# Where the recurrence's outputs are transposed, and which engine scales P: a two-layer decoder kernel

## The chip, the cores and the metric

The kernel runs on one core of one Trainium2 chip. The metric is the device time of one execution in microseconds (us), lower is better. The core has TensorE (PE, matmuls; PEld is its weight loading), VectorE (DVE), ScalarE (ACT), GpSimd (POOL) and a queue for DMA issues on SyncE (SP). Each engine works through its own instructions in a fixed order and waits on semaphores for the others.

## What is computed

Two layers of a decoder trunk on one sequence of 512 tokens, 1024 wide, in float32. In each layer an RWKV-7 recurrence (8 heads of 64) and a latent attention (MLA, 8 heads) run on the same normalised input; their outputs are gated, added and projected, and a gated MLP with a short convolution follows. Cut to what the change touches:

```python
y = _wkv7_scan(r, decay, k, v, -kk, kk * iclr)            # recurrence, (tokens, 8 heads, 64)
mu = jnp.mean(y, axis=-1, keepdims=True)                  # group norm over the 64 of a head
var = jnp.mean(jnp.square(y - mu), axis=-1, keepdims=True)
y = (y - mu) * lax.rsqrt(var + LNX_EPS) * lnx_w + lnx_b
y_a = ((y + bonus) * gate) @ w_out_rwkv

s = (q_nope @ k_nope.T + q_pe @ k_pe.T) * scale           # attention, causal mask
p = jax.nn.softmax(s, axis=-1)
y_b = (p @ v) @ w_out_mla

merged = sigmoid(gate_a) * y_a + sigmoid(gate_b) * y_b
h = h + merged @ w_out
```

## The kernel before

**Layout and products.** Activations lie transposed, features on the 128 partitions and the 512 tokens along the free axis. A large product is made of three matmuls (`mm3`, L253 to L255): both operands are split into a high and a low part in the fp32r format, and high x high, low x high and high x low are summed in PSUM. Weights come as units of 128 x 1024 from HBM over SP's queue (`produce`, L211), into two buffers each for the raw, high and low parts; ScalarE makes the high part (L203) and VectorE the low one (L204). `unit` keeps two units ready ahead of use. Activations are split in the same way by `split` (L286 on ScalarE, L287 on VectorE).

**Stages of a layer** (`mixer`). First the input projections, with the preparation of the recurrence for four pairs of heads. Then the recurrence over eight half-chunks of 64 tokens. Then the part in which the change lies, and last the output projections and the MLP.

**The part around the change** runs these functions in this order, once a layer:

- `outputs`: for four chunks of 128 tokens, `chunk_out(i)` sums the outputs of all heads in the two-bank PSUM tile xy, of which there is a single buffer (matmuls L874 and L884), and ScalarE copies them to Z (L888).
- `norms`: for each chunk, `group_norm(i)` has VectorE sum each head's 64 values (L896), multiply the sums by 1/64 (L897) and subtract them (L898); ScalarE squares (L899), VectorE sums the squares (L900) and scales (L901), and GpSimd raises to the power -0.5 (L902). `group_scale` then multiplies Z on GpSimd (L907).
- `heads(p)`, four times, each for a pair of heads: the key projection (3 matmuls) is copied by ScalarE (L957) and completed by GpSimd (L958), the two query projections (12 matmuls) are scaled by VectorE (L965). For four blocks of 128 queries and two heads: scores on TensorE (L973), masking and row minimum of the negated scores on VectorE (L976), exp with row sums on ScalarE (L979), reciprocal on VectorE (L980), scaling of P by it on ScalarE (L981), up to four 128 x 128 transposes on TensorE (L984), and a copy of the turned P out of PSUM (L985), on ScalarE for blocks 1 and 3 and on VectorE for blocks 0 and 2. At the end 16 matmuls give P x V (L992), and the result is split.
- `transposed`, between the second and the third pair: four calls of `yop`, two to an xy tile. Each transposes 128 features of all four chunks (four L913), loads the bonus and the gate (L915, L917) into two rotating buffers that all four calls share, adds the transposed values times lnx_w to the bonus (L923, or two halves at L921 for the last two calls), multiplies by the gate (L924) and splits the result.

After the four pairs come eight products of all four split outputs with w_out_rwkv, each followed by a multiplication with the gate (L1005).

**What sets the order.** The order on each engine is fixed when the kernel is built. A scheduler goes by priority, which is the order in the program, and puts later work ahead of earlier work where the earlier isn't ready by its own reckoning. Only the stretches inside `manual_schedule` keep TensorE's order as written. So the place of `transposed` in the list of functions sets a rank, not a fixed place. The accumulators of the projections have two PSUM buffers, keys and queries five buffers in SBUF, P three.

Of the kernel before, what the change touches and what calls it, by code (L numbers as in the profile page):

```python
# [9 lines left out]
F32 = mybir.dt.float32  # L10
F32R = mybir.dt.float32r
I32 = mybir.dt.int32
AF = mybir.ActivationFunctionType
ALU = mybir.AluOpType
# [145 lines left out]
def build(ctx, tc, x, pos, wst, vecd, constd, out):  # L160
    nc = tc.nc
    V, A, G, PE = nc.vector, nc.scalar, nc.gpsimd, nc.tensor
# [270 lines left out]
    def mixer(l, ops, nrm, wks):  # L433
        with ExitStack() as mx:
# [245 lines left out]
            with pool(name=f"ti{l}", bufs=2) as ti, tc.manual_schedule(engines={PE.engine}):  # L680
# [130 lines left out]
                for c in range(8):  # L811
                    i, e = divmod(c, 2)
                    xy = xyt()
# [16 lines left out]
                    for hd in (0, 4, 1, 5, 2, 6, 3, 7):  # L830
                        s, ur, vr = slot(c, hd // 2)
                        g, n = divmod(hd, 4)
# [24 lines left out]
            with pool(name=f"tb{l}", bufs=2) as tb:  # L857
# [7 lines left out]
                def chunk_out(i):  # L865
                    xy = xyt()
                    begun, left = set(), {(r, hh): 4 for r in (0, 64) for hh in range(2)}
                    for p in range(4):
                        for e, hh in ((0, 0), (1, 1), (0, 1), (1, 0)):
                            c = 2 * i + e  # L870
                            s, ur, vr = slot(c, p)
                            k0 = 64 * hh
                            if c:
                                PE.matmul(xy[vr:vr + 64, hh, 64 * p:64 * p + 64], AR[p][k0:k0 + 64, s, vr:vr + 64],  # L874
                                          St[c][k0:k0 + 64, p, :], start=(vr, hh) not in begun, stop=False,
                                          tile_position=(k0, vr))
                                begun.add((vr, hh))
                    for hh in range(2):
                        for p in range(4):
                            for e in range(2):  # L880
                                s, ur, vr = slot(2 * i + e, p)
                                hd = 2 * p + hh
                                left[vr, hh] -= 1
                                PE.matmul(xy[vr:vr + 64, hh, 64 * p:64 * p + 64], AM[:, hd, s, vr:vr + 64],  # L884
                                          Z[:, i, e, 64 * hd:64 * hd + 64], start=(vr, hh) not in begun,
                                          stop=left[vr, hh] == 0, tile_position=(0, vr))
                                begun.add((vr, hh))
                    A.copy(Z[:, i, 0, :].rearrange("p (q h i) -> p q h i", h=2, i=64),  # L888
                           xy[:, :, 0:256].rearrange("p h (q i) -> p q h i", i=64))


                def group_norm(i):
                    Y = Z[:, i, 0, :].rearrange("p (h i) -> p h i", i=64)
                    s2 = Z[:, i, 1, :].rearrange("p (h i) -> p h i", i=64)
                    mu = tb.tile([128, 16], F32, name="mu", bufs=4)
                    V.tensor_reduce(mu[:, 0:8], Y, mybir.AxisListType.X, ALU.add)  # L896
                    V.tensor_scalar(mu[:, 0:8], mu[:, 0:8], 1.0 / 64, None, ALU.mult)  # L897
                    V.tensor_tensor(Y, Y, mu[:, 0:8, None].to_broadcast([128, 8, 64]), ALU.subtract)  # L898
                    A.activation(s2, Y, AF.Square)  # L899
                    V.tensor_reduce(mu[:, 8:16], s2, mybir.AxisListType.X, ALU.add)  # L900
                    V.tensor_scalar(mu[:, 8:16], mu[:, 8:16], 1.0 / 64, LNX_EPS, ALU.mult, ALU.add)  # L901
                    G.tensor_tensor(mu[:, 0:8], mu[:, 8:16], mhalf[:, 0:8], ALU.pow)  # L902
                    return mu[:, 0:8]
# [7 lines left out]
                def yop(ps, p):  # L911
# [12 lines left out]
                    V.tensor_tensor(bl, bl, gt, ALU.mult)  # L924
                    yops.append(split(xp, bl, None, "xa", 8))

                def outputs():
                    for i in range(4):
                        chunk_out(i)

                def norms():
                    for i, gr in enumerate([group_norm(i) for i in range(4)]):
                        group_scale(i, gr)

                def transposed():
# [15 lines left out]
                def heads(p):  # L951
# [8 lines left out]
                    for hh in range(2):  # L960
# [3 lines left out]
                        q = MT("q", "qk", 5)  # L964
# [3 lines left out]
                    PTs = [tb.tile([128, 13, 128], F32, name="PT", tag="PT", bufs=4) for _ in range(2)]  # L968
                    for b in range(4):
                        n = 128 * (b + 1)  # L970
                        for hh in range(2):
                            sp = sc()
                            PE.matmul(sp[:, 0:n], qs[hh][:, 128 * b:128 * b + 128], ks[hh][:, 0:n], start=True, stop=True)  # L973
                            P = MT("P", "P")
# [3 lines left out]
                                                   scalar=1e30, op0=ALU.add, op1=ALU.min, accum_out=mn[:, 0:1])  # L978
                            A.activation(P[:, 0:n], P[:, 0:n], AF.Exp, bias=mn[:, 0:1], scale=-1.0, accum_out=mn[:, 1:2])  # L979
                            V.reciprocal(mn[:, 2:3], mn[:, 1:2])  # L980
                            A.activation(P[:, 0:n], P[:, 0:n], AF.Copy, scale=mn[:, 2:3])  # L981
                            pt = pb.tile([128, 512], F32, name="pt", tag="pt")
                            for kb in range(b + 1):
                                PE.transpose(pt[:, 128 * kb:128 * kb + 128], P[:, 128 * kb:128 * kb + 128], ident)  # L984
                            (A.copy if b % 2 else V.tensor_copy)(PTs[hh][:, b:4 * b + 1:3, :],  # L985
                                                                 pt[:, 0:n].rearrange("p (k q) -> p k q", q=128))

                    with tc.manual_schedule(engines={PE.engine}):
# [5 lines left out]
                                          start=kb == 0, stop=kb == 3, tile_position=(0, 64 * hh))  # L994
                    oops.append(split(xp, po, None, "xb", 8))

                for f in (outputs, norms, lambda: heads(0), lambda: heads(1), transposed, lambda: heads(2), lambda: heads(3)):
                    f()

                gas = []  # L1000
# [151 lines left out]
```

## Time and profile before

| what | us |
|---|---|
| median of 3 runs | 1564.96 |
| lowest and highest | 1563.26, 1566.88 |
| the profiled execution: its time | 1565.82 |
| its span in the trace | 1564.0 |
| PE busy | 1532.7 (98%) |
| DVE busy | 913.5 (58%) |
| ACT busy | 669.2 (43%) |
| POOL busy | 184.4 (12%) |

The shares are means over the whole span, and most of it is large products that feed TensorE alone. The stage around the change takes from about 278 to 338 us in layer 0 and again from about 1050 to 1110 us in layer 1; only there do all engines work on one chain. A row of a wait names the engine, the tile and line that waited, the engine, tile and line that ended the wait, then the total, the number of times and the longest. A row of a time window gives its length and the busy time of PE, PEld, DVE, ACT and POOL with the numbers of their instructions, then the clock granted to TensorE as a share of full speed, the share of DMA time and the GB/s.

### The profile page before, as it was taken

What the parts mean: (1) busy time and instruction counts of PE and PEld (TensorE: products, weight loads), DVE (VectorE), ACT (ScalarE), POOL (GpSimd) and SP (SyncE); (2) the same over time, 40 slices, a digit from 0 to 9 for tenths busy, and PEclk for the clock granted to TensorE, in tenths of its full rate; (3) what the DMA queues carried; (4) which work ended last, traced back from release to release, by engine and by line L of the source; (5) the groups of instructions that cost most, each with busy time, mean ns of one, the idle gap of its engine ahead of it and who ended that gap; (6) DMA issues with size and microseconds to landing.
All of it is one profiled execution on the core that took longest, in us unless ns stands there. A gap on an engine that the chain in (4) does not pass through costs nothing.

```text
span 1564.0 us, 22128 instructions
## 1 busy us (share of the span) xinstructions
PE 1532.7 (98%) x8860; PEld 1233.0 (79%) x8860; DVE 913.5 (58%) x1510; ACT 669.2 (43%) x1020; POOL 184.4 (12%) x157
## 2 busy tenths in 40 slices
PE   8999999999999999999999999998999999999998
PEld 6888886668888888888878888765788888888887
DVE  6579795766555555533346768867564555554332
ACT  6445444663443333322244544457444333333222
POOL 1011101300311110100001121013012111100000
PEclk9999999999999999999999999999999999999999
DMA  6324322324323222333342333222352232222322
GB/s 208 115 95 139 124 83 69 96 86 155 122 89 101 95 95 94 100 116 115 108 149 94 109 108 117 81 65 92 101 171 92 96 106 95 94 95 96 103 98 81
DMA packets 57270, 166.05 MB, mean 106 GB/s; under 512 B 6352, under 2 KB 8528, under 8 KB 57168
## 3 DMA queue, kind: packets, MB, share of 16 engines
q1 hardware_dynamic: 57024, 164.48, 31.9%
q8 instruction: 69, 1.13, 0.3%
q14 instruction: 33, 0.27, 0.1%
q10 hardware_dynamic: 144, 0.16, 0.0%
HBM read 147.32 MB, written 17.30 MB: 105 GB/s over the span
## 4 chain that ended last, share of the span: by engine, by line
PE 92%; DVE 5%; ACT 1%; issue 1%; POOL 0%; DMA 0%; DVEq 0%; POOLq 0%; SPq 0%; ACTq 0%
PE acc L253 27%; PE acc L254 27%; PE acc L255 27%; PE sc L973 2%; PE pt L984 1%; PE po L992 1%; PE m L635 1%; DVE wlo L204 1%; PE xy L834 1%; PE m L643 1%; PE xy L844 1%; PE acc L947 1%; PE m L540 0%; DVE X L694 0%; DVE tm L692 0%
## 5 line engine op out<-in xcount | busy, mean ns | idle before, releaser
L253 PE MATMUL acc<-hi,whi 128*128 128x512 f32 (+1 forms) x1918 | 755.0, 394 | 6.1 <-ACT hi L289 5.2
L255 PE MATMUL acc<-hi,wlo 128*128 128x512 f32 (+1 forms) x1918 | 747.4, 390 | 0.8 <-DVE wlo L204 0.8
L254 PE MATMUL acc<-lo,whi 128*128 128x512 f32 (+1 forms) x1918 | 746.8, 389 | 0.0
L203 ACT CAST whi<-raw 128x1024 fp32r<-128x1024 f32 (+2 forms) x249 | 253.4, 1019 | 535.8 <-PE acc L254 463.3
L253 PEld LDWEIGHTS acc<-hi,whi 128*128 128x128 f32 x1918 | 361.2, 188 | 81.4 <-ACT hi L289 5.2
L255 PEld LDWEIGHTS acc<-hi,wlo 128*128 128x128 f32 x1918 | 361.2, 188 | 75.4 <-DVE wlo L204 1.3
L254 PEld LDWEIGHTS acc<-lo,whi 128*128 128x128 f32 x1918 | 361.5, 188 | 71.1 <-DVE lo L290 0.5
L204 DVE TENSOR_TENSOR wlo<-raw,whi 128x1024 fp32r<-128x1024 f32 (+2 forms) x249 | 303.3, 1220 | 178.2 <-ACT whi L203 177.8
L1072 POOL TENSOR_TENSOR c<-c,rstd 128x512 f32<-128x512 f32 x44 | 57.9, 1317 | 403.6 <-ACT c L1071 403.6
L1065 DVE TENSOR_TENSOR u<-acc,rstd 128x512 f32<-128x512 f32 x44 | 30.4, 692 | 104.4 <-PE acc L255 104.3
L1074 DVE TENSOR_TENSOR c<-c,acc 128x512 f32<-128x512 f32 x44 | 30.2, 687 | 86.4 <-POOL c L1072 86.4
L1071 ACT ACTIVATE c<-c 128x512 f32<-128x512 f32 x44 | 27.8, 632 | 81.7 <-DVE c L1070 81.7
L312 POOL TENSOR_TENSOR nv<-nv,cst 128x4 f32<-128x4 f32 (+1 forms) x10 | 10.0, 996 | 335.4 <-DVE nv L311 335.4
L348 POOL TENSOR_TENSOR nacc<-nacc,nsq 128x512 f32<-128x512 f32 x14 | 25.1, 1790 | 193.0 <-ACT nsq L347 193.0
L973 PE MATMUL sc<-K,q 128*128 128x128 f32 (+3 forms) x128 | 45.4, 451 | 1.3 <-DVE mn L976 1.0
L466 DVE TENSOR_TENSOR cur<-acc,rstd 128x512 f32<-128x512 f32 x28 | 19.1, 689 | 45.1 <-PE acc L255 37.6
L981 ACT ACTIVATE P<-P,mn 128x128 f32<-128x128 f32 (+3 forms) x64 | 35.1, 559 | 5.1 <-DVE mn L980 4.8
L979 ACT ACTIVATE P<-P,mn 128x128 f32<-128x128 f32 (+3 forms) x64 | 35.5, 556 | 3.7 <-DVE mn L976 3.5
L1068 ACT ACTIVATE c<-u,vec 128x512 f32<-128x512 f32 x44 | 35.7, 811 | 2.8 <-DVE u L1064 2.8
L976 DVE CUSTOM_DVE_ANT_0 P<-sc,cst 128x128 f32<-128x128 f32 (+3 forms) x64 | 30.4, 482 | 8.1 <-PE sc L973 5.5
L1070 DVE SCALAR_TENSOR_TENSOR c<-u,vec,c 128x512 f32<-128x512 f32 x44 | 33.1, 752 | 1.5
L1069 DVE SCALAR_TENSOR_TENSOR c<-u,vec,c 128x512 f32<-128x512 f32 x44 | 32.8, 746 | 1.8 <-ACT c L1068 1.8
(243 smaller groups left out, 1318.5 us busy)
## 6 DMA issues: line engine op xcount, KB each, us to landing
raw<-in_w SPq DMA_DIRECT2D x238, 512.0 KB, 3.3
gate_d<-gg SPq DMA_DIRECT2D x32, 256.0 KB, 2.0
AM<-gate_d SPq DMA_DIRECT2D x16, 256.0 KB, 4.2
gb<-gate_d SPq DMA_DIRECT2D x16, 256.0 KB, 3.2
h<-in_x SPq DMA_DIRECT2D x8, 256.0 KB, 4.3
rgate_d<-gt SPq DMA_DIRECT2D x8, 256.0 KB, 2.5
bl_d<-rk SPq DMA_DIRECT2D x8, 256.0 KB, 4.2
bl<-bl_d SPq DMA_DIRECT2D x8, 256.0 KB, 2.6
```

Of the source, the lines that this page charges most:

```text
L203: A.copy(hi, r)
L204: V.tensor_tensor(lo, r, hi.bitcast(F32), ALU.subtract)
L253: PE.matmul(ps, w[0], xx[0], start=first, stop=False)
L254: PE.matmul(ps, w[0], xx[1], start=False, stop=False)
L255: PE.matmul(ps, w[1], xx[0], start=False, stop=last)
L973: PE.matmul(sp[:, 0:n], qs[hh][:, 128 * b:128 * b + 128], ks[hh][:, 0:n], start=True, stop=True)
L979: A.activation(P[:, 0:n], P[:, 0:n], AF.Exp, bias=mn[:, 0:1], scale=-1.0, accum_out=mn[:, 1:2])
L981: A.activation(P[:, 0:n], P[:, 0:n], AF.Copy, scale=mn[:, 2:3])
L1068: A.activation(cc, u[:, 2:514], AF.Identity, bias=vc(l, "conv_b", i), scale=vc(l, "conv_w", 2 * FT + i))
L1069: V.scalar_tensor_tensor(cc, u[:, 1:513], vc(l, "conv_w", FT + i), cc, ALU.mult, ALU.add)
L1070: V.scalar_tensor_tensor(cc, u[:, 0:512], vc(l, "conv_w", i), cc, ALU.mult, ALU.add)
L1072: G.tensor_tensor(cc, cc, rstd, ALU.mult)
```

## The change

Three edits, all in the part described above.

1. `transposed` is called behind `heads(2)` and no longer behind `heads(1)`.
2. The sums for the group norm's means are taken by VectorE straight from the PSUM tile xy in `chunk_out`, beside ScalarE's copy, and no longer from Z. The multiplication of the sums by -1/64 and the subtraction become one operation.
3. The scaling of P by the reciprocal is a `tensor_scalar` on VectorE and no longer an activation on ScalarE, and all copies of the turned P are made by ScalarE.

```diff
@@ chunk_out
+                    mu = tb.tile([128, 16], F32, name="mu", bufs=4)
+                    V.tensor_reduce(mu[:, 0:8].rearrange("p (q h) -> p h q", h=2),
+                                    xy[:, :, 0:256].rearrange("p h (q i) -> p h q i", i=64), mybir.AxisListType.X, ALU.add)
                     A.copy(Z[:, i, 0, :].rearrange("p (q h i) -> p q h i", h=2, i=64),
                            xy[:, :, 0:256].rearrange("p h (q i) -> p q h i", i=64))
+                    return mu
@@ group_norm
-                def group_norm(i):
+                def group_norm(i, mu):
-                    mu = tb.tile([128, 16], F32, name="mu", bufs=4)
-                    V.tensor_reduce(mu[:, 0:8], Y, mybir.AxisListType.X, ALU.add)
-                    V.tensor_scalar(mu[:, 0:8], mu[:, 0:8], 1.0 / 64, None, ALU.mult)
-                    V.tensor_tensor(Y, Y, mu[:, 0:8, None].to_broadcast([128, 8, 64]), ALU.subtract)
+                    V.scalar_tensor_tensor(Y, mu[:, 0:8, None].to_broadcast([128, 8, 64]), -1.0 / 64, Y, ALU.mult, ALU.add)
@@ outputs, norms
+                sums = []
+
                 def outputs():
                     for i in range(4):
-                        chunk_out(i)
+                        sums.append(chunk_out(i))
 
                 def norms():
-                    for i, gr in enumerate([group_norm(i) for i in range(4)]):
+                    for i, gr in enumerate([group_norm(i, sums[i]) for i in range(4)]):
                         group_scale(i, gr)
@@ heads
                             V.reciprocal(mn[:, 2:3], mn[:, 1:2])
-                            A.activation(P[:, 0:n], P[:, 0:n], AF.Copy, scale=mn[:, 2:3])
+                            V.tensor_scalar(P[:, 0:n], P[:, 0:n], mn[:, 2:3], None, ALU.mult)
...
-                            (A.copy if b % 2 else V.tensor_copy)(PTs[hh][:, b:4 * b + 1:3, :],
+                            A.copy(PTs[hh][:, b:4 * b + 1:3, :],
@@ the order
-                for f in (outputs, norms, lambda: heads(0), lambda: heads(1), transposed, lambda: heads(2), lambda: heads(3)):
+                for f in (outputs, norms, lambda: heads(0), lambda: heads(1), lambda: heads(2), transposed, lambda: heads(3)):
```

## The prediction

> **What bounds the kernel now.** I read the page first (the chain that ended last, then the costliest groups), then who waited for whom on TensorE, then time windows over the stage in which the change lies, and last its timeline.
>
> ```profile
> PE 92%; DVE 5%; ACT 1%; issue 1%; POOL 0%; DMA 0%; DVEq 0%; POOLq 0%; SPq 0%; ACTq 0%
> PE xy L913 <- POOL Z L907: 4.0, 2, 2.0
> PE pt L984 <- DVE mn L980: 1.7, 2, 0.8
> PE xy L874 <- ACT Z L888: 1.6, 4, 0.6
> PE sc L973 <- DVE mn L976: 1.0, 2, 0.5
> PE xy L913 <- DVE bl L921: 0.9, 2, 0.5
> ```
>
> TensorE carries 92% of the chain, so an edit on another engine is worth only what it takes from TensorE's idle or slow time. The waits (total, times, longest) fall in equal halves on the two layers, all in the stage that the change touches. Layer 0's stage, from the end of the second pair's projections to the last pair, in thirds (length; busy PE, PEld, DVE, ACT, POOL; clock):
>
> ```profile
> 290.00:306.00 16.00, 13.93 (x67) 10.25 (x66) 12.80 (x38) 11.61 (x29) 6.12 (x6) 0.89 0.21 67
> 306.00:322.00 16.00, 14.07 (x72) 8.27 (x70) 12.42 (x39) 13.26 (x33) 0.61 (x1) 1.00 0.24 66
> 322.00:338.00 16.00, 16.00 (x86) 9.62 (x85) 10.23 (x31) 11.87 (x29) 0.00 (x0) 1.00 0.16 47
> ```
>
> TensorE is idle for 2.07 us in the first third and 1.93 us in the second, and runs at 0.89 clock in the first (0.11 x 16 = 1.8 us lost). The last third is full: there the products with the recurrence's output weights fill the holes of the last pair. ScalarE (13.26 of 16) is the busiest of the helpers in the second third, VectorE (12.80) in the first. One microsecond at a time, the first third shows:
>
> ```profile
> 290.00:291.00 1.00, 0.37 (x3) 0.13 (x1) 0.86 (x4) 0.00 (x0) 1.00 (x1) 1.00 0.00 0
> 291.00:292.00 1.00, 0.00 (x0) 0.00 (x0) 1.00 (x4) 0.63 (x1) 0.92 (x2) 1.00 0.00 0
> 293.00:294.00 1.00, 1.00 (x5) 0.76 (x4) 0.93 (x5) 0.30 (x1) 0.48 (x1) 0.62 0.00 0
> 294.00:295.00 1.00, 1.00 (x5) 0.80 (x4) 0.25 (x2) 0.78 (x2) 1.00 (x1) 0.50 0.00 0
> 295.00:296.00 1.00, 1.00 (x3) 0.60 (x3) 0.43 (x1) 1.00 (x3) 0.92 (x2) 0.50 0.00 0
> 296.00:297.00 1.00, 1.00 (x3) 0.46 (x3) 1.00 (x1) 0.91 (x4) 0.28 (x1) 0.67 0.00 0
> ```
>
> The transposes (L913) stand in TensorE's queue ahead of work that could run, wait 2.0 us for GpSimd's scaling of Z, and just behind that the clock is at half for some three microseconds. Both belong to one event.
>
> **Part 1: the transposes move behind pair 2.** The function issues 16 transposes, 8 loads on SP's queue, 6 VectorE steps on the transposed data (two of 0.73 us, four halves), four products with the gate, and four splits. None goes away; all now rank behind pair 2's work, which takes TensorE and VectorE first. Where the transposes stood, pair 2's 15 projection matmuls can run, which need nothing from the norms. So the wait of 2.0 us goes (a) and with it the slow clock, 1.8 us (b). What is late next is the end of the outputs' own chain, since the products at the end need all four:
>
> ```profile
> 297.89 0.73 DVE L923 SCALAR_TENSOR_TENSOR bl<-xy,vec,bl 128x512 f32<-128x512 f32 x1
> 302.00 0.69 DVE L965 TENSOR_TENSOR q<-acc,rq 128x512 f32<-128x512 f32 x1
> 306.87 2.37 PE L992 MATMUL po<-PT,Vt 128*64 128x512 f32 x16
> 322.12 2.37 PE L992 MATMUL po<-PT,Vt 128*64 128x512 f32 x16
> 323.20 0.62 ACT L286 CAST hi<-bl 128x512 fp32r<-128x512 f32 x1 [0.85 <-DVE bl L924]
> 323.85 0.69 DVE L287 TENSOR_TENSOR lo<-bl,hi 128x512 fp32r<-128x512 f32 x1 [0.22 <-ACT hi L286]
> 328.85 0.79 PE L253 MATMUL acc<-hi,whi 128*128 128x512 f32 x1
> 319.68 0.32 SPq L917 DMA_DIRECT2D rg<-rgate_d  x1
> 322.48 0.68 DVE L924 TENSOR_TENSOR bl<-bl,rg 128x512 f32<-128x512 f32 x1
> 322.59 13.98 SPq L211 DMA_DIRECT2D raw<-in_w  x2
> DMA to landing us min/median/max: 2.6/2.7/3.9
> ```
>
> The chain runs from 297.89 to 324.54, 26.65 us. The fourth output is first used by the matmul at 328.85: 4.3 us of slack. The two buffers of loads set its pace (the last gate's load is issued at 319.68, when a buffer comes free, and its product follows at 322.48, the 2.7 us of a landing later). The delay lies between nothing (the transposes find holes at once) and one pair, 322.12 - 306.87 = 15.25 us. I take 6, nearer the low end: in before pair 2's projections were done at 302.00, 4.1 us behind the chain's start, and its first scores come behind them. That costs 6 - 4.3 = 1.7 us (e), with ends 0 and 10.9. On SP's queue, which is worked in order, the next weights (322.59) come behind the last gate load; a load that waits longer for its buffer holds them back too. I put nothing on it: here the weights were issued 2.9 us behind that load, and the code keeps two units of weights ready ahead of use.
>
> **Part 2: the scaling of P to VectorE, the copies of turned P to ScalarE.** Eight scalings for a pair of heads, four copies of each of the two kinds.
>
> ```profile
> L981 ACT ACTIVATE P<-P,mn 128x128 f32<-128x128 f32 (+3 forms) x64 | 35.1, 559 | 5.1 <-DVE mn L980 4.8
> L985 DVE COPY PT<-pt 128x384 f32<-128x384 f32 x16 | 8.8, 552 | 1.6 <-PE pt L984 1.5
> L985 DVE COPY PT<-pt 128x128 f32<-128x128 f32 x16 | 4.6, 286 | 3.4 <-PE pt L984 3.2
> L985 ACT COPY PT<-pt 128x512 f32<-128x512 f32 x16 | 9.4, 585 | 0.8 <-PE pt L984 0.6
> L985 ACT COPY PT<-pt 128x256 f32<-128x256 f32 x16 | 5.9, 369 | 3.4 <-PE pt L984 3.3
> L374 DVE TENSOR_SCALAR ang<-pf,cst 128x512 f32<-128x512 f32 x2 | 1.0, 484 | 0.0
> L897 DVE TENSOR_SCALAR mu<-mu 128x8 f32<-128x8 f32 x8 | 1.4, 169 | 0.1
> ```
>
> ScalarE loses 8 x 0.559 = 4.47 us for a pair. On the line through its two copies (0.369 at 256, 0.585 at 512) the new ones are 0.26 and 0.48, so 2 x 0.74 = 1.48 comes: net -3.0. VectorE has a multiply by a column at 0.484 for 512 and the same operation at 0.169 for 8; on that line 128, 256, 384 and 512 take 0.24, 0.32, 0.40 and 0.48, twice 1.46 = 2.9. It loses 2 x (0.286 + 0.552) = 1.68: net +1.24. Queued behind each new scaling on VectorE are the next tile's minimum and the projections' epilogues. The 1.93 us idle of the second third arises where ScalarE is the fullest; of its relief of 3.0 VectorE takes 1.24 back, so I credit 59% of 1.93, 1.1 us (c), with ends 0 and 1.93.
>
> **Part 3: the means from PSUM.** For each chunk of four:
>
> ```profile
> L896 DVE TENSOR_REDUCE mu<-Z 128x8 f32<-128x512 f32 x8 | 5.4, 676 | 0.0
> L898 DVE TENSOR_TENSOR Z<-Z,mu 128x512 f32<-128x512 f32 x8 | 5.5, 692 | 0.5
> L1070 DVE SCALAR_TENSOR_TENSOR c<-u,vec,c 128x512 f32<-128x512 f32 x44 | 33.1, 752 | 1.5
> ```
>
> The small multiply goes (0.17), the subtraction becomes a step like L1070 (+0.06), the sum read from PSUM costs at most what the PSUM-fed 0.73 us step above does (+0.05). VectorE gains 0.06 us a chunk: nothing. The sum now runs beside ScalarE's copy, but the single xy buffer stays taken until both have read it, so the next chunk's matmuls gain a second wait: 0 to 0.68 us for each of three. Behind a waiting chunk stand, on TensorE, pair 0's turns and products and pair 1's scores, and ScalarE and VectorE wait for these. TensorE waits there 0.8 us a layer for ScalarE's copy; with the scalings gone from ScalarE I credit half, 0.4 us (d), ends 0.8 and -1.2.
>
> **Sum.** a 2.0 + b 1.8 + c 1.1 + d 0.4 - e 1.7 = 3.6 us a layer, 7.2 us in all. The profiled execution took 1565.82 us (span 1564.0, 1.8 around it), 0.86 above the median of 1564.96; I take 7.2 off the median: 1557.8 us.
>
> **Rivals.** *The outputs come too late (slower).* If TensorE is so well fed by pair 2 that the transposes wait a whole pair, the fourth output is 10.9 us late behind the slack. An uncrowded chain is shorter by at most 26.65 - 16.8 (three steps of landing 2.7, split 1.3, product 0.69, and 2.7 at its ends), so between 10.9 and, with half of that saved, 6.0 us are lost: 8.5. Against gains of 5.3 that is 3.2 a layer, 1571.4 us. It makes the kernel measurably slower (1.6 us a layer) from a loss of 6.9, that is from outputs 11.2 us later than in before. For it: the order is fixed when the kernel is built, and holes there may be other holes than on the chip. Against it: in before fillers ran two pairs ahead.
>
> *VectorE takes ScalarE's place (no change).* VectorE was busy 12.80 of 16; 1.24 comes. And a multiply by a column can stall while GpSimd works:
>
> ```profile
> 172.86 2.03 POOL L606 TENSOR_TENSOR BKb<-BK,z 128x512 f32<-128x512 f32 x1
> 173.91 1.27 DVE L620 TENSOR_SCALAR rk<-rk,vec 128x512 f32<-128x512 f32 x1
> L620 DVE TENSOR_SCALAR rk<-rk,vec x8: 472/474/1270, 83.6 to 945.7; 128x512 f32<-128x512 f32 x8
> ```
>
> It took 1.27 us instead of 0.474 beside GpSimd. GpSimd is busy 6.12 of 16 in the first third, so 3 of a pair's 8 scalings would pay 0.8 each, 2.4 us: VectorE would need 12.80 + 1.24 + 2.4 = 16.4 of 16. Then a and b go into its queue, and 1.1 + 0.4 - 1.7 = -0.2 a layer is left: 1565.4 us. Against it: GpSimd does 0.61 in the second third. The Trainium skill says of this (SBUF — State Buffer, "Who interferes with whom") that such a VectorE operation and a GpSimd one hold a shared port pair in turn and the later blocks fully; the 1.27 agrees.
>
> *The move does nothing.* The fixed order may fill the same holes with the same transposes; a, b and e are 0, c and d leave 3.0 us: 1562.0.
>
> *The slow clock has another cause.* The tensor work was loose from 285 on, and b may stay when the 2.0 us gap goes: 1557.8 + 3.6 = 1561.4 us. The Trainium skill's rule (TensorE: Matmul & The Clock Gate, "HAM oscillation — how this bites in real kernels") is that gaps above some 3.4 us throttle; by it 2.0 us would not. The 0.50 straight behind the gap speaks against it here.
>
> **Numbers.** A measurement of this kernel tells 0.2%, 3.1 us, from no change. Chances: forecast 0.50, late outputs 0.14, VectorE 0.18, no move 0.10, clock 0.08. Faster: 0.46 + 0.01 + 0.05 + 0.05 = 0.57 (forecast, VectorE, no move, clock); same: 0.04 + 0.11 + 0.05 + 0.03 = 0.23; slower: late outputs 0.14 and 0.06 of VectorE. The range's low end is all idle and slow time recovered, 2 x (2.0 + 1.8 + 1.93 + 0.8) = 13.1: 1552; its high end, 1568, holds all but late outputs and VectorE's bad part. The forecast's own range is 1552 to 1561.9.
>
> **What would show it.** Right: no wait of L913 for GpSimd, clock 1.00 around 290 to 300, ScalarE near 10 of 16 in the middle third, scalings near 0.24 to 0.48 us, the matmul with the fourth output before 328.85. Wrong: the final products waiting for the splits (L287) or for loads, VectorE above 15 of 16 there, scalings above 0.8 us beside GpSimd, or a slow clock without a gap.

## The result, and the profile after

| kernel | median, us | lowest to highest | runs | the profiled execution | its span | its clock |
|---|---|---|---|---|---|---|
| before | 1565.92 | 1563.26 to 1567.81 | 4 | 1565.82 | 1564.0 | 0.994 |
| after | 1556.1 | 1555.94 to 1557.86 | 4 | 1556.17 | 1554.3 | 0.998 |

The changed kernel is faster by 9.8 us: 0.9937 of the time before, interval 0.9925 to 0.9949. The forecast was 1557.8 us, 7.2 us less than the median of before that was known then (1564.96; a fourth run has moved it by 1.0). Line numbers in the part of the change are larger by 1 to 3 in the new kernel (power L903, scaling of Z L908, transposes L914, product with the gate L925, scores L976 and minimum L979, scaling of P L984, turns L987, copies L988, P x V L995); the sum from PSUM is L889, ScalarE's copy of xy L891.

The chain that ended last, by engine:

```profile
PE 90%; DVE 6%; ACT 2%; issue 1%; DMA 0%; SPq 0%; POOL 0%; DVEq 0%; POOLq 0%
```

TensorE still carries it. Of the five waits of TensorE that were quoted of before, three are gone: no L914 waits for GpSimd or for VectorE's step that reads the transposed data (L922), and L874 no longer waits for ScalarE's copy. What TensorE waits for there now (total, times, longest, both layers):

```profile
PE pt L987 <- ACT PT L988: 1.0, 2, 0.5
PE sc L976 <- DVE mn L979: 0.6, 2, 0.3
PE pt L987 <- DVE P L984: 0.5, 2, 0.3
PE sc L976 <- DVE q L968: 0.3, 1, 0.3
```

These are steps of the softmax itself: the turns wait 0.5 us for the scaling, where in before they waited 1.7 us for the reciprocal ahead of it, and the scores 0.6 us for the minimum instead of 1.0. No wait is above 0.5 us. The three thirds of layer 0's stage, and the whole of it (length; busy PE, PEld, DVE, ACT, POOL; clock; DMA):

```profile
290.00:306.00 16.00, 15.64 (x79) 9.31 (x78) 15.19 (x46) 12.19 (x31) 7.46 (x6) 1.00 0.21 67
306.00:322.00 16.00, 15.22 (x83) 10.14 (x83) 15.19 (x46) 10.91 (x30) 1.13 (x1) 1.00 0.30 99
322.00:338.00 16.00, 16.00 (x80) 11.04 (x79) 9.50 (x24) 8.33 (x18) 0.00 (x0) 1.00 0.29 99
275.00:351.00 76.00, 74.62 (x593) 52.29 (x588) 58.02 (x153) 41.99 (x101) 14.27 (x11) 1.00 0.29 98
```

TensorE's idle time is 0.36 us in the first third (before 2.07) and 0.78 in the second (before 1.93), and the clock is full. VectorE is busy for 15.19 of 16 us in both. The last row stands against this one of before:

```profile
275.00:351.00 76.00, 71.18 (x572) 49.55 (x568) 52.93 (x147) 49.93 (x116) 12.55 (x11) 0.98 0.29 91
```

In the same 76 us TensorE does 3.4 us more, at a clock higher by 0.02 (some 1.5 us). VectorE has 5.1 us more work, ScalarE 7.9 less; a part of both is that after's stage is over within these 76 us and before's is not.

How long the whole stage is, can be read between two anchors that both kernels have: the last L834 of the recurrence, and the first product with the attention's gate. In layer 0 (a row is: start, length, instruction, idle time before it and what ended it), before and after:

```profile
274.62 0.56 PE L834 MATMUL xy<-xs,AM 64*64 64x64 f32 x12
356.18 0.69 DVE L1026 SCALAR_TENSOR_TENSOR gb<-gb,acc 128x512 f32<-128x512 f32 x1 [0.64 <-PE acc L255]
```

```profile
274.69 0.51 PE L834 MATMUL xy<-xs,AM 64*64 64x64 f32 x10
350.91 0.69 DVE L1029 SCALAR_TENSOR_TENSOR gb<-gb,acc 128x512 f32<-128x512 f32 x1 [0.64 <-PE acc L255]
```

81.56 us have become 76.22; in layer 1, 81.51 have become 76.42. Together that is 10.4 us, more than the spans differ by (9.7).

### The profile page after: what moved, and what is told of

Read it like the earlier page. It is cut to its first block, busy times and chain, and to the rows that moved or that the text cites. A ratio compares the mean times of both kernels' runs of the same rounds, so it can differ in the third digit from the quotient of the medians.

```text
span 1554.3 us, 22132 instructions
## 1 busy us (share of the span) xinstructions
PE 1529.7 (98%) x8860; PEld 1230.2 (79%) x8860; DVE 925.2 (60%) x1534; ACT 651.0 (42%) x988; POOL 187.7 (12%) x157
## 4 chain that ended last, share of the span: by engine, by line
PE 90%; DVE 6%; ACT 2%; issue 1%; DMA 0%; SPq 0%; POOL 0%; DVEq 0%; POOLq 0%
PE acc L253 27%; PE acc L254 26%; PE acc L255 26%; PE sc L976 1%; PE pt L987 1%; PE m L635 1%; PE po L995 1%; DVE wlo L204 1%; PE xy L834 1%; PE m L643 1%; PE xy L844 1%; PE acc L950 1%; PE m L540 0%; ACT whi L203 0%; DVE xs L826 0%
## 5 line engine op out<-in xcount | busy, mean ns | idle before, releaser
L976 PE MATMUL sc<-K,q 128*128 128x128 f32 (+3 forms) x128 | 44.1, 444 | 1.2 <-DVE mn L979 0.6
L982 ACT ACTIVATE P<-P,mn 128x128 f32<-128x128 f32 (+3 forms) x64 | 35.8, 561 | 6.8 <-DVE mn L979 5.7
L988 ACT COPY PT<-pt 128x128 f32<-128x128 f32 (+3 forms) x64 | 27.1, 424 | 21.4 <-PE pt L987 20.4
L987 PE MATMUL pt<-cst,P 128*128 128x128 f32 x160 | 31.1, 286 | 1.8 <-ACT PT L988 1.0
```

## Experiments

The theory: the move takes away the wait for GpSimd and the slow clock with it (a and b of the sum), and the softmax edit pays by relieving ScalarE (c and d). The rivals: the softmax edit is worth something only where VectorE's longer queue is covered (*cover*); the outputs come too late; VectorE is the new bound.

For each kernel the table gives, from its one profile, the time from the first L834 of the recurrence to the end anchor above, both layers together. A period of slow clock (3.4 us at half speed in the traces) takes some 1.65 us of it. In eight cases a kernel has such a period in one layer's stage or recurrence and none in the other layer's, and the one with it is longer by 1.25 to 1.96 us, 1.6 on average. The third column counts those that the profile has, the fourth leaves them out, and the fifth compares what is left with before. The recurrence has to be counted in, since kernels with the softmax edit do more of pair 0's turns within it (in layer 0 13 instead of 9, by the groups of L987 and L984 there), so that the border between the two shifts by some 1 us.

| kernel | recurrence and stage, 2 layers | slow periods | without them | against before | measured ratio, interval |
|---|---|---|---|---|---|
| before | 246.3 | 4 | 239.7 | | |
| after | 236.2 | 1 | 234.6 | -5.2 | 0.9937 [0.9925, 0.9949] |
| move_only | 239.4 | 2 | 236.1 | -3.7 | 0.9944 [0.9932, 0.9956] |
| softmax_only | 247.5 | 1 | 245.9 | +6.2 | 1.0023 [1.0015, 1.0032] |
| means_only | 241.4 | 0 | 241.4 | +1.7 | 0.9981 [0.9973, 0.9990] |
| no_move | 244.2 | 2 | 240.9 | +1.2 | 0.9999 [0.9991, 1.0008] |
| no_softmax | 240.9 | 3 | 236.0 | -3.8 | 0.9963 [0.9950, 0.9976] |
| no_means | 238.5 | 0 | 238.5 | -1.3 | 0.9963 [0.9948, 0.9977] |
| last | 239.9 | 2 | 236.6 | -3.1 | 0.9955 [0.9944, 0.9967] |
| half_scale | 240.4 | 1 | 238.8 | -0.9 | 0.9958 [0.9946, 0.9970] |
| scale_only | 242.3 | 3 | 237.4 | -2.4 | 0.9972 [0.9960, 0.9985] |
| copies_only | 248.0 | 3 | 243.1 | +3.4 | 1.0015 [1.0005, 1.0025] |
| gate_pool | 240.8 | 1 | 239.1 | -0.6 | 0.9966 [0.9952, 0.9981] |
| two_two | 236.0 | 2 | 232.7 | -7.0 | 0.9928 [0.9911, 0.9946] |

One profile a kernel is little, but every run has its span and its mean granted clock on record, so the split can be repeated roughly over all runs: (1 - clock) x span is what the slow clock took, the rest is work. The slow clock took 8.5 us in before on average (62 runs of these sessions), 3.5 in after, 4.1 in move_only, 4.3 in means_only, 6.4 in softmax_only, 8.4 in no_softmax and 5.2 in no_means. The work differs from before's by -5.2, -4.0, +1.4, +5.9, -4.8 and -2.6 us for these six in this order, within 1.4 us of the table. (Before's own work is 1556.3 to 1556.8 us in each of the three sessions, so that after, measured in another session, can be set against it.)

### move_only: the order of the functions alone

```diff
# on the kernel before
-                for f in (outputs, norms, lambda: heads(0), lambda: heads(1), transposed, lambda: heads(2), lambda: heads(3)):
+                for f in (outputs, norms, lambda: heads(0), lambda: heads(1), lambda: heads(2), transposed, lambda: heads(3)):
```

> The kernel of before with the transposes called behind the third pair, and nothing else. Theory 'move and relief' (mine): the two parts add; the move alone takes away the wait for GpSimd (2.0 us a layer) and the slow clock behind it (1.8), so 7 to 8 us faster than before. Rival 'relief': ScalarE's load in the softmax is what holds the stage, the move alone is worth at most 2 us. Rival 'interaction': the move alone gives 0 to 3 us, since VectorE and ScalarE then queue the outputs' steps later in a full ScalarE; only with the softmax edit does it pay.

Measured: 1558.32 us against 1566.59 for before, 8.3 less. TensorE's waits in layer 0's stage:

```profile
PE pt L984 <- DVE PT L985: 1.8, 3, 1.1
PE xy L874 <- ACT Z L888: 0.8, 2, 0.6
PE pt L984 <- ACT PT L985: 0.2, 1, 0.2
```

The wait of L913 is gone; what is next is pair 2's own turns, which wait for the copies of the turns before them, 1.8 us in three pieces. The wait for ScalarE's copy (0.8) is as in before. The clock in the stage is full in both layers. So the move brings most of the gain by itself, slightly more than the 7 to 8 us expected: 3.7 us of work in the table's terms, and 3.3 of slow clock in the stage, 7.0 of the 8.3. By the ratios it can't be told from after at all (0.9944 [0.9932, 0.9956] and 0.9937 [0.9925, 0.9949]). The second third of its stage:

```profile
306.00:322.00 16.00, 15.08 (x81) 9.95 (x79) 14.02 (x42) 12.87 (x32) 0.61 (x1) 1.00 0.34 103
```

TensorE is idle for 0.92 us there, where before had 1.93, though ScalarE still does all the scalings and is busy for 12.87 us.

### softmax_only: the scaling to VectorE and the copies to ScalarE alone

```diff
# on the kernel before
-                            A.activation(P[:, 0:n], P[:, 0:n], AF.Copy, scale=mn[:, 2:3])
+                            V.tensor_scalar(P[:, 0:n], P[:, 0:n], mn[:, 2:3], None, ALU.mult)
...
-                            (A.copy if b % 2 else V.tensor_copy)(PTs[hh][:, b:4 * b + 1:3, :],
+                            A.copy(PTs[hh][:, b:4 * b + 1:3, :],
```

> The kernel of before with P scaled on VectorE and turned P copied by ScalarE, and nothing else. 'Move and relief': 2 to 5 us faster (the idle of the second third, 1.9 us a layer, and the waits for ScalarE's copy of the outputs, 0.8), while the transposes still wait some 2 us for GpSimd. 'Relief': 7 us or more faster. 'Interaction': 0 to 3 us.

Measured: 1570.77 us against 1566.59, 4.2 us *more*. The expectation of a gain failed. The timeline of the last chunk's norm in layer 0 shows why; first before, then this kernel:

```profile
291.81 0.69 DVE L900 TENSOR_REDUCE mu<-Z 128x8 f32<-128x512 f32 x1
293.28 0.16 DVE L901 TENSOR_SCALAR mu<-mu 128x8 f32<-128x8 f32 x1
293.52 1.64 POOL L902 TENSOR_TENSOR mu<-mu,cst 128x8 f32<-128x8 f32 x1 [1.22 <-DVE mu L901]
295.23 1.04 POOL L907 TENSOR_TENSOR Z<-Z,mu 128x512 f32<-128x512 f32 x1
297.38 0.27 PE L913 MATMUL xy<-cst,Z 128*128 128x128 f32 x1
```

```profile
293.10 0.67 DVE L900 TENSOR_REDUCE mu<-Z 128x8 f32<-128x512 f32 x1
294.76 0.56 DVE L976 CUSTOM_DVE_ANT_0 P<-sc,cst 128x384 f32<-128x384 f32 x1 [0.92 <-PE pt L984]
295.24 0.17 DVE L901 TENSOR_SCALAR mu<-mu 128x8 f32<-128x8 f32 x1
295.72 0.61 POOL L958 COPY K<-kp 64x512 f32<-64x512 f32 x1 [3.17 <-PE sc L973]
296.41 1.64 POOL L902 TENSOR_TENSOR mu<-mu,cst 128x8 f32<-128x8 f32 x1
298.12 1.04 POOL L907 TENSOR_TENSOR Z<-Z,mu 128x512 f32<-128x512 f32 x1
299.22 0.33 PE L913 MATMUL xy<-cst,Z 128*128 128x128 f32 x1 [2.33 <-POOL Z L907]
```

The norms go through VectorE's queue between the softmax steps. With the scalings in that queue its order is another one: ahead of the variance's scaling (L901) stands a minimum (L976) at which VectorE is idle for 0.92 us, and L901 starts at 295.24 and no longer at 293.28. GpSimd's order has the completion of a key (L958) in front of the power by now, and the power starts at 296.41 instead of 293.52. So Z comes 2.9 us later, and as long as the transposes stand behind pair 1, TensorE waits for it, in each of the two layers:

```profile
PE xy L913 <- POOL Z L907: 3.5, 2, 2.3
```

That is 1.5 us a layer more than the 2.0 of before, 3.0 of the 6 us of work that this kernel loses; waits for ScalarE's copies of the turned P, 1.4 us a layer, are new too. The first is the wait that the prediction set out to remove, and the softmax edit lengthens the chain that feeds it.

### means_only and no_move: the other edit alone, and the two edits without the move

```diff
# means_only: the kernel before with edit 2 of the change and nothing else
# no_move: the kernel after, with
-                for f in (outputs, norms, lambda: heads(0), lambda: heads(1), lambda: heads(2), transposed, lambda: heads(3)):
+                for f in (outputs, norms, lambda: heads(0), lambda: heads(1), transposed, lambda: heads(2), lambda: heads(3)):
```

> The kernel of before with the means summed from PSUM, and nothing else. 'Move and relief': within 1.5 us of before. Rival 'norm chain': each chunk's norm is ready some 0.8 us earlier, the wait of the transposes for GpSimd shrinks by that, 1.5 to 4 us faster.

> The changed kernel with the transposes called behind the second pair again (means from PSUM and both softmax edits stay). 'Move and relief': 2 to 5 us faster than before, 5 to 8 slower than the changed kernel, with the wait for GpSimd and the slow clock back. 'Relief': within 2 us of the changed kernel. 'Norm chain': within 2 us of the changed kernel too, since the wait is mostly gone without the move.

Measured: means_only 1564.59, no_move 1566.72, before 1566.59 us. The means alone give 2.0 us, and by the table all of that is clock: the work takes 1.7 us more, but no slow period fell into its profile. Its eleven runs bear that out (4.3 us of slow clock a run against 8.5). L914's waits there are 1.8 us a layer, in two pieces of at most 1.0. For no_move 2 to 5 us less than before were expected; without the move the two edits are worth nothing (0.9999 [0.9991, 1.0008]). So the move is what the change needs.

no_move also shows how the slow clock comes. The transposes wait for GpSimd in layer 0 and in layer 1, each time 2.12 us:

```profile
299.08 0.33 PE L914 MATMUL xy<-cst,Z 128*128 128x128 f32 x1 [2.12 <-POOL Z L908]
1069.66 0.33 PE L914 MATMUL xy<-cst,Z 128*128 128x128 f32 x1 [2.12 <-POOL Z L908]
```

The 5 us straight behind each (the clock is the third number from the right):

```profile
300.00:305.00 5.00, 4.35 (x20) 3.38 (x18) 3.68 (x7) 1.68 (x4) 0.00 (x0) 0.66 0.46 146
1070.00:1075.00 5.00, 4.10 (x26) 2.78 (x27) 4.16 (x8) 2.17 (x4) 0.28 (x1) 1.00 0.34 116
```

One gap is followed by 0.66 (0.34 x 5 = 1.7 us lost), its twin by full speed. Such a gap brings the slow clock often, not always.

### no_softmax and no_means: the change without one of its other edits

```diff
# no_softmax: the kernel after, with
-                            V.tensor_scalar(P[:, 0:n], P[:, 0:n], mn[:, 2:3], None, ALU.mult)
+                            A.activation(P[:, 0:n], P[:, 0:n], AF.Copy, scale=mn[:, 2:3])
...
-                            A.copy(PTs[hh][:, b:4 * b + 1:3, :],
+                            (A.copy if b % 2 else V.tensor_copy)(PTs[hh][:, b:4 * b + 1:3, :],
# no_means: the kernel before, with the move and the softmax edit, without edit 2
```

> The changed kernel with both softmax edits taken back (move and means stay). The move alone gave 8.3 us, the means alone about 2 to 3, the softmax edits alone cost about 4. Theory 'the parts add': this is 10.5 to 12 us faster than before, 1.5 to 4 faster than the changed kernel. Theory 'cover' (mine): the softmax edits cost only where the transposes wait for norms that VectorE then delivers later; behind the move the norms have time, the loss is gone and ScalarE's relief pays: this is 1 to 4 us slower than the changed kernel, 6 to 9 faster than before.

> The kernel of before with the move and the softmax edits, the means taken from Z as before. 'The parts add': 4 to 5 us faster than before. 'Cover': 7.5 to 10.5 faster than before, within 2.5 us of the changed kernel, since norms that are ready earlier are worth nothing once the transposes come later.

Measured: 1562.67 and 1560.43 us, 4.2 and 6.4 less than before, 0.9963 of it for both, where after has 0.9937. Both of *cover*'s forecasts were missed (6 to 9 and 7.5 to 10.5 less). With the means in place the softmax edit brings about 0.26% (4 us) that it cost when alone. But move_only, which has neither edit, stands at 0.9944. So behind the move the kernel with one of the two edits is some 3 us slower than with none (the intervals just overlap), and with both it is 1.1 us faster, which can't be told from nothing. *Cover* isn't borne out as it was meant: the move alone doesn't make the softmax edit pay.

no_softmax's profile is some 6 us behind after's where the recurrence ends (last L834 at 280.75 and 274.69), so its first two thirds are taken 6.06 us later:

```profile
296.06:312.06 16.00, 14.21 (x77) 9.09 (x77) 12.80 (x39) 13.37 (x32) 6.52 (x6) 1.00 0.20 68
312.06:328.06 16.00, 15.75 (x81) 9.88 (x80) 12.27 (x41) 14.84 (x39) 0.61 (x1) 1.00 0.31 95
```

ScalarE is the full one again in the second third, but TensorE is busy for 15.75 us of it, more than in after (15.22): ScalarE's load there isn't what costs. What is missing is in the first third, 14.21 us against 15.64, and there TensorE waits for the scaling of Z again, first in layer 0, then in layer 1:

```profile
PE xy L914 <- POOL Z L908: 1.1, 1, 1.1
PE xy L914 <- POOL Z L908: 1.3, 1, 1.3
```

Counted from the last L834, the transposes begin after 20.3 us in no_softmax and after 22.7 in after, and the last scaling of Z ends at 22.4 and at 22.8. So the later rank alone does not keep the wait away; it depends on where the rebuilt order puts the transposes. Of the 4 us the table accounts for 1.4 of work and, with two slow periods more in the one profile, 3.3 of clock; over all runs it is 0.9 and 4.9.

For no_means the expectation, within 2.5 us of after, was missed: the means are worth 0.26% too once the other two edits are there, while they cost 1.7 us of work alone. TensorE waits there, in each layer, 1.2 us for copies of the turned P, 0.7 for scalings, 0.4 for ScalarE's copy of xy and 0.2 for a minimum. That is 5.0 us in both layers, where after has 2.5; the table has 3.9 us of work between the two. The order on every engine is worked out anew for each kernel, and which of the moved steps brings these waits was not found.

### last and two_two: where the transposes rank

```diff
# last: the kernel after, with
+                for f in (outputs, norms, lambda: heads(0), lambda: heads(1), lambda: heads(2), lambda: heads(3), transposed):
# two_two: the kernel after, with two of the four outputs behind each of the last two pairs
-                def transposed():
-                    for p in range(0, 4, 2):
+                def transposed(ps2=(0, 2)):
+                    for p in ps2:
...
+                for f in (outputs, norms, lambda: heads(0), lambda: heads(1), lambda: heads(2), lambda: transposed((0,)),
+                          lambda: heads(3), lambda: transposed((2,))):
```

> The changed kernel with the transposes called behind the fourth pair. The prediction's rival 'outputs too late' (mine): one more pair of delay uses up the slack, the products wait for the fourth output and TensorE runs out of filler in the last pair: 2 to 6 us a layer, 4 to 12 slower than the changed kernel, with waits of the products for the splits of bl. Rival 'rank hardly matters': the transposes find the same holes, within 2 us of the changed kernel.

> The changed kernel with two of the four transposed outputs behind the third pair and two behind the fourth. Behind the second pair it was 10.6 us slower than the changed kernel, behind the fourth 3.6 slower. 'Outputs too late' (mine): the last two are as late as with all four behind the fourth pair, 2 to 4 us slower than the changed kernel. Rival 'room': the first two find their holes, the last two leave VectorE to the third pair, within 1.5 us or faster.

Measured: last 1559.75, two_two 1556.13 us. One more pair's delay for all four outputs costs some 3 us (0.9955 [0.9944, 0.9967], which just overlaps with after's interval), less than the 4 to 12 expected: in last the fourth output's split begins only at 330.43, after has it at 322.88, and so there is less to fill the holes of the last pair with. The last third of its stage:

```profile
322.00:338.00 16.00, 15.11 (x77) 10.31 (x76) 11.23 (x27) 7.68 (x17) 0.00 (x0) 1.00 0.36 108
```

TensorE is idle for 0.89 us, where before and after are full. With half of them held back nothing is lost: two_two's last split begins at 327.55 and its stage is 0.6 to 1.0 us a layer shorter than after's. The expectation that its outputs would be too late was wrong. Its middle third:

```profile
306.00:322.00 16.00, 15.74 (x84) 10.08 (x84) 15.43 (x52) 12.75 (x36) 1.14 (x1) 1.00 0.32 96
```

TensorE is idle for 0.26 us there, after for 0.78. The measured times of two_two and after can't be told apart (0.9928 [0.9911, 0.9946], 0.9937 [0.9925, 0.9949]). Both beat before; none beats after for sure.

### half_scale, scale_only, copies_only, gate_pool: who has how much

```diff
# each: the kernel after, with one edit
# half_scale: the scaling for blocks 0 and 2 back on ScalarE
+                            (V.tensor_scalar(P[:, 0:n], P[:, 0:n], mn[:, 2:3], None, ALU.mult) if b % 2 else
+                             A.activation(P[:, 0:n], P[:, 0:n], AF.Copy, scale=mn[:, 2:3]))
# scale_only: the copies shared as in before
+                            (A.copy if b % 2 else V.tensor_copy)(PTs[hh][:, b:4 * b + 1:3, :],
# copies_only: all scalings on ScalarE, and all copies too
+                            A.activation(P[:, 0:n], P[:, 0:n], AF.Copy, scale=mn[:, 2:3])
# gate_pool: the outputs' product with the gate on GpSimd
-                    V.tensor_tensor(bl, bl, gt, ALU.mult)
+                    G.tensor_tensor(bl, bl, gt, ALU.mult)
```

> The changed kernel with the scaling of blocks 0 and 2 on ScalarE again (blocks 1 and 3 on VectorE; all copies of turned P by ScalarE). If VectorE, 15.2 us busy of 16 in the changed kernel, now holds the stage ('VectorE bound'): 1 to 4 us faster than the changed kernel. If TensorE's own work bounds it ('TensorE bound', mine): within 1.5 us.

> The changed kernel with the copies of turned P shared between ScalarE and VectorE as before; P is scaled on VectorE. VectorE gets 1.7 us a pair back. 'VectorE is full' (mine): 2 to 6 us slower than the changed kernel, since VectorE is busy 15.2 of 16 us in the first two thirds there. Rival 'only the handing over counts' (P scaled by the engine that makes the reciprocal saves a hop to ScalarE, the copies don't matter): within 1.5 us of the changed kernel.

> The changed kernel with P scaled on ScalarE as before, and all copies of turned P by ScalarE too. ScalarE gets 4.5 us a pair back, VectorE loses 2.9. 'The load of the fuller engine counts' (mine): ScalarE would need some 16 us a pair and bounds the stage, 5 to 12 us slower than the changed kernel. 'Only the handing over counts': 3 to 5 us slower, as without the softmax edits.

> The changed kernel with the product of the outputs and the gate on GpSimd instead of VectorE, four of 0.69 us a layer. 'VectorE is full' says it bounds the stage: 1 to 3 us faster than the changed kernel. 'TensorE bound' (what is left is TensorE's own work, 1.4 us idle a layer): within 1.5 us. A product on GpSimd takes some 1.3 us and stalls VectorE's scalings beside it, up to 0.8 each; if that weighs more, 1 to 3 us slower.

Measured: 1560.54, 1563.19, 1569.11 and 1560.88 us; each is slower than after, by about 3, 5.5, 12 and 4.5 us when the ratios are compared (half_scale's interval just overlaps with after's). For half_scale a time within 1.5 us of after or a faster one was expected, and that was missed; scale_only (2 to 6 us slower) and copies_only (5 to 12) came as expected. copies_only puts the most on ScalarE, and TensorE then waits for it, and again for the norms (rows of one layer; the other has the same):

```profile
PE pt L987 <- ACT P L984: 1.4, 2, 1.2
PE xy L914 <- POOL Z L908: 1.8, 1, 1.8
```

scale_only puts the most on VectorE (15.54 us of the first third), and a query that VectorE has to scale comes late:

```profile
290.00:306.00 16.00, 14.02 (x78) 8.74 (x76) 15.54 (x47) 10.48 (x27) 7.84 (x7) 1.00 0.15 54
```

1.98 us of TensorE are idle there, 1.9 of them one wait of L976 for the scaled query (L968). gate_pool was meant as the test of VectorE as the bound. It takes VectorE down to 13.43 of 16 in the middle third, and the kernel gets slower:

```profile
306.00:322.00 16.00, 14.79 (x76) 8.88 (x75) 13.43 (x42) 10.61 (x28) 4.21 (x4) 1.00 0.29 99
```

It is no clean test, since the edit also does what was feared of it: GpSimd's product takes 1.27 us where VectorE's takes 0.69, and scalings beside it are stretched, three of layer 0's. One of them, 1.00 us where a scaling of 128 takes 0.28 to 0.29 elsewhere:

```profile
300.84 1.27 POOL L925 TENSOR_TENSOR bl<-bl,rg 128x512 f32<-128x512 f32 x1 [1.87 <-issue]
301.20 1.00 DVE L984 TENSOR_SCALAR P<-P,mn 128x128 f32<-128x128 f32 x1
```

two_two says more: its VectorE is fuller than after's in the middle third (15.43 of 16), and TensorE is busier all the same (15.74 against 15.22). So a VectorE that is 95% busy is not by that what sets the time. That what counts is when single steps of its queue come, and which of them wait behind GpSimd, fits all these kernels but is not shown by itself, since the order is worked out anew in all of them. None of these four divisions beats after's.

## Why the prediction was right

The cause that carries the forecast, the move, is shown by move_only and no_move. The division of the gain was not right, and that the total came near is partly luck. For the move (a + b - e) the sum had 2.1 us a layer; move_only measured 8.3 us, 4.15 a layer. For the rest (c + d) it had 1.5 a layer; what after gains beyond move_only is 1.1 us by the ratios, some 0.55 a layer, and can't be told from nothing. The two errors offset each other.

**The wait (a) and the slow clock (b).** Forecast 3.8 us a layer. Both went, in both layers. move_only shows it alone: 1.85 us a layer of work and 1.65 of clock. Over all runs the slow clock took 8.5 us in before and 4.1 in move_only. The rival *the move does nothing* (1562.0) falls with that kernel, whose gain of 8.3 us is more than the whole forecast, and so does *another cause of the slow clock* (1561.4): b had to stay in it, and no stage in move_only's and after's profiles has a slow period. The size of b was right for a layer that has a slow period, but it isn't a fixed price of the gap: no_move had the same gap in both layers and paid once.

**ScalarE's relief (c and d).** Forecast 1.5 us a layer. The reason given for c was wrong. It was worked out of the 1.93 us that TensorE was idle in the second third, put down to a full ScalarE; in move_only, with all scalings still on ScalarE, 0.92 are left, and in after 0.78. So nearly all of what c was to bring came from the move. softmax_only relieves ScalarE in the same way and loses 4.2 us, because the norms share VectorE's queue. The prediction looked at what is queued behind the scalings on VectorE, and named the next tile's minimum and the epilogues; it left out the norms' steps (L896 to L901). The wait for ScalarE's copy of xy (d) is gone entirely, 0.8 us a layer instead of the half that was credited. The credited half was right for the softmax edit: in softmax_only and no_means 0.4 us a layer of this wait are left. In means_only, no_softmax and after none is left, so the other half went with the means, from which the prediction expected a wait more.

**The means.** Forecast nothing. The operations came out no dearer than forecast; in groups of after,

```profile
L889 DVE TENSOR_REDUCE mu<-xy 128x8 f32<-128x512 f32 x8 | 5.5, 688 | 2.7 <-PE xy L884 2.7
L899 DVE SCALAR_TENSOR_TENSOR Z<-mu,Z 128x512 f32<-128x512 f32 x8 | 5.5, 692 | 2.4 <-ACT Z L891 2.4
```

the sum takes 0.688 (before 0.676) and the merged step 0.692, as long as the subtraction did. The second reader of xy that was feared, up to 0.68 us for each of three chunks, doesn't show: L874 waits for neither. But with both other edits the means are worth about 4 us (no_means), and with the move alone they cost perhaps 3 (no_softmax against move_only): a term that depends on the other edits, which the sum lacked.

**The late outputs (e).** This term was mis-sized: 1.7 us a layer were taken off, and nothing was lost. The chain's first step, and the last split of it:

```profile
300.07 0.75 DVE L924 SCALAR_TENSOR_TENSOR bl<-xy,vec,bl 128x512 f32<-128x512 f32 x1
322.88 0.69 DVE L287 TENSOR_TENSOR lo<-bl,hi 128x512 fp32r<-128x512 f32 x1
```

The chain begins 2.2 us later than in before (297.89), not 6, and takes 23.5 us instead of 26.65, so that it ends at 323.57, before even the old end at 324.54. A rank one pair later meant 2 us: the order fixed at build time put the transposes into holes ahead of their rank. The rival *too late* (1571.4) needed 11.2 us. Even last, with the outputs behind all four pairs, ends its chain 6.6 us later than before (331.12) and still beats before.

**VectorE takes ScalarE's place.** The load came as feared, 15.19 of 16 us, the time did not. The scalings of P in after, by their length:

```profile
L984 DVE TENSOR_SCALAR P<-P,mn 128x384 f32<-128x384 f32 x16 | 7.8, 490 | 0.3
L984 DVE TENSOR_SCALAR P<-P,mn 128x512 f32<-128x512 f32 x16 | 7.7, 480 | 0.1
L984 DVE TENSOR_SCALAR P<-P,mn 128x256 f32<-128x256 f32 x16 | 6.8, 427 | 0.4
L984 DVE TENSOR_SCALAR P<-P,mn 128x128 f32<-128x128 f32 x16 | 4.4, 285 | 0.3
```

Forecast 0.40, 0.48, 0.32 and 0.24. Some meet work of GpSimd; the longest, beside GpSimd's scaling of Z:

```profile
288.08 1.05 POOL L908 TENSOR_TENSOR Z<-Z,mu 128x512 f32<-128x512 f32 x1
288.33 0.94 DVE L984 TENSOR_SCALAR P<-P,mn 128x256 f32<-128x256 f32 x1
```

0.94 us in place of some 0.35. On the line through the means at 128 and 512, 256 and 384 would take 0.35 and 0.415; the excess is (0.427 - 0.35 + 0.49 - 0.415) x 16 = 2.4 us, or 0.3 for each of the eight passes of a pair through the stage. The rival feared 2.4 for one pair in the first third. Of three such collisions a pair, fewer than one came: three scalings a layer took 0.62 us or more, each while GpSimd was working. Two of the signs that the prediction gave for being wrong came, VectorE above 15 of 16 and a scaling above 0.8 us, without the loss they were to stand for.

**The sum.** Forecast 3.6 us a layer. Measured by the profiles 2.6 of work and 1.65 of clock, 4.25 a layer or 8.5 in all. Before's profile has one slow period more in the recurrence than after's, which makes 10.1 in the two profiled executions; it lies outside what the change touches, and the medians' 9.8 may hold a part of it too.

## What to carry to other kernels

Where an in-order engine stands at a wait with runnable work behind it, give the waiting step a later rank, and price the delay by the slack of its last consumer; the delay can be much less than the distance in rank. Do that first: here it brought nearly all of the gain. An edit that moves work between two helper engines can change sign with what else is changed, since another chain may stand in the helper's queue behind the moved step: the softmax edit cost 4 us alone, perhaps 3 behind the move, and brought 4 behind the move and the means. Price edits together, not one by one: here -3.7, +6.2 and +1.7 us of work apart made -5.2 together. And when the sum comes out, test its largest part alone: a total can be near with its parts wrong.

## What the runs showed of the hardware

In the stage and in the recurrence the slow clock comes in periods of one size, about 3.4 us at half speed, some 1.65 us lost, and not every time. Of 28 passes through the stage (14 profiles, two layers), 10 had a single TensorE wait of 1.7 us or more. In 5 of these a slow period came right behind it. In the two passes of copies_only one came too, but some 20 us later, behind a wait of 1.19 us. Of the 18 others one had a slow period, in no_softmax, behind a wait of 1.26 us. In the recurrence the longest wait is 1.0 us, and 17 of 28 passes had a slow period. Before and after have the same waits there; 5 us of it, first before, then after:

```profile
250.00:255.00 5.00, 3.88 (x45) 2.74 (x47) 1.33 (x4) 0.95 (x2) 1.22 (x2) 0.73 0.62 210
```

```profile
250.00:255.00 5.00, 3.38 (x60) 2.48 (x57) 1.71 (x5) 1.33 (x3) 1.22 (x2) 1.00 0.74 254
```

With four such places in an execution, two in the stage and two in the recurrence, the clock alone can part two executions of one kernel by several steps of 1.65 us; the 4.6 us between the shortest and the longest run of before would be about three. The runs without a profile don't show the places, but they fit: of the 62 runs of before in the experiments' sessions, the 13 with a mean clock of 0.993 have a mean span of 1566.7 us, the 5 with 0.997 one of 1562.7. The Trainium skill (TensorE: Matmul & The Clock Gate, "HAM oscillation — how this bites in real kernels") puts the danger at gaps above some 3.4 us. No gap in these stretches was that long, and half clock came behind gaps of 1.2 to 2.3 us and in a stretch with none above 1.0. So by these runs the clock can fall without such a gap; what brings it in the recurrence, the thin filling of some of its 5 us or something else, isn't shown.
